# A row maximum that ignores NaN on one core: the loads of tiles 6 to 60 split into two halves on two DMA queues

## The chip, the core and the metric

The kernel runs on one core of a Trainium2 chip. Four engines matter. VectorE (DVE) does the reductions, ScalarE (ACT) and GpSimd (POOL) do passes over the elements, SyncE (SP) issues DMAs; the core's 16 DMA engines carry the transfers between the memory of the chip (HBM) and the on-chip memory (SBUF). TensorE is not used. Each engine runs its own list of instructions in order, and engines wait for each other on semaphores. The metric is the device time of one execution in microseconds; before the change it is 1252.5 us (median of 3 runs, 1252.5 to 1252.64).

## What is computed

```python
batch, seq, dim = 32, 2048, 2048
x = np.random.randn(batch, seq, dim).astype(np.float32)
mask = np.random.rand(batch, seq, dim) < 0.1
x[mask] = np.nan

def reference(x, axis):            # axis is -1
    return np.nanmax(x, axis=axis).astype(np.float32)
```

There are 65,536 rows of 2048 float32, 537 MB in all, of which a tenth is NaN. The result is the largest number of each row with the NaNs left out, 65,536 numbers. Every element is read once from HBM.

## The kernel before, in words

**Tiles.** The input is cut into tiles that hold, in each of the 128 partitions, a run of whole or quarter rows: `Q = 512` elements is the unit, and a full tile has 28 of them per partition (7 rows, 57344 bytes in a partition, 7168 KB in all). `TILES` (line 16) lists for each tile its loads, its pieces and its reductions, in units. Tile 1 is small (4 units), tiles 2 to 62 are full and each come with one load, and from tile 63 on the loads are cut into ever smaller parts, so that little work is left after the last one. Tiles are numbered from 1 in this text.

**The work on a tile.** A NaN has to be taken out before the maximum. Three steps do that, each with its own engine:
- ACT makes keys: for each piece it reads the upper 16 bits of every element as int16 and writes a u16 key into one of three key buffers `kt` (line 384). The function is a Prelu whose two slopes map bit patterns of numbers and of NaNs onto separate ranges.
- POOL turns the keys back and writes them over the upper 16 bits in the tile `xt` (line 405), which leaves NaNs as bit patterns that lose in a maximum. A negative number of units in the list of pieces means that ACT does this step too for that piece (`held` and `release`, line 357); in the middle of the kernel this is so in one tile of eight, the first of them tile 9.
- DVE reduces whole rows of the tile to their maxima in `acc` (line 430).

In the profile all of ACT's and all of POOL's passes have the line of their helper (L222, L232), and DVE's reductions have L239.

**Rows without a number.** A row of NaNs alone would keep a value at the lower end; `find` (line 241) corrects such entries of `acc` in one pass on DVE (L245), with `acc` as both tensor inputs. It is called behind tile 60 for 414 columns and behind the last tile for 7. For the fifth group `find_late` (line 256) does it on POOL in two instructions.

**Buffers and order.** Three tile buffers `xt` and three key buffers `kt` are used in turn. `Order` writes the waits: each instruction raises a semaphore of its engine (a DMA one of its own lane by 16), and `add` puts a wait before an instruction for each dependency that the engine has not yet seen. Each engine's list is in the order in which the Python code adds to it. A load waits for `free` of its buffer (line 311), which is the last reduction of the tile three before it:

```python
xt, before = xts[number % BUFS], free[number % BUFS]
...
free[(number - 1) % BUFS] = after[-1:]
```

All loads and the stores at the end are issued by SP, in order, on SP's queue. The first piece of a tile waits for the load that holds it. A key pass waits for POOL, where the key buffer that it writes is still being read (`kold`).

Of the kernel before, what the change touches and what calls it, by code (L numbers as in the profile page):

```python
# [10 lines left out]
Q = D // 4  # L11
# [38 lines left out]
GROUPS = [TILES[i : i + 15] for i in range(0, 60, 15)] + [TILES[60:73], TILES[73:]]  # L50
# [3 lines left out]
LATE = 4  # L54
# [3 lines left out]
BUFS = 3  # L58
# [4 lines left out]
LEAD = 128  # L63

LANES = 14

# [9 lines left out]
def total(pieces):  # L78
    return sum(sum(map(abs, p)) if isinstance(p, tuple) else abs(p) for p in pieces)
# [93 lines left out]
def kernel(  # L173
# [15 lines left out]
    nc = tc.nc  # L189
    P = nc.NUM_PARTITIONS  # L190
    f32, i32 = mybir.dt.float32, mybir.dt.int32
    i16, u16 = mybir.dt.int16, mybir.dt.uint16
    ALU = mybir.AluOpType
# [6 lines left out]
    xr = x.bitcast(i32).flatten_outer_dims()  # L200
    R = xr.shape[0]
    of = out.bitcast(i32).flatten_outer_dims().rearrange("r c -> (r c)")
    rows = [sum(sum(loads) for loads, _, _ in g) * Q // D for g in GROUPS]
    assert R == P * sum(rows)

    sing = ctx.enter_context(tc.tile_pool(name="sing", bufs=1))

    scalars = sing.tile([P, LEAD // 4], f32, name="scalars")
    warm = scalars[:, 1:2]
    xts = [sing.tile([P, WIDE * D], i32, name=f"xt{i}") for i in range(BUFS)]  # L210
    kts = [sing.tile([P, KEYS], u16, name=f"kt{i}") for i in range(NKEYS)]
    accs = sing.tile([P, sum(rows)], f32, name="acc")
    late = sing.tile([P, rows[LATE]], i32, name="late")

    with tc.tile_critical():  # L215
# [25 lines left out]
        def find(deps, acc):  # L241
            return order.add(
                "dve",
                nc.vector,
                lambda: nc.vector.scalar_tensor_tensor(  # L245
                    out=acc,
                    in0=acc,
                    scalar=LEAST,
                    in1=acc,
                    op0=ALU.is_ge,  # L250
                    op1=ALU.mult,
                ),
                deps,
            )

        def find_late(deps, acc, none):
            e = order.add(
                "pool",
                nc.gpsimd,
                lambda: nc.gpsimd.tensor_scalar(  # L260
                    out=none,
                    in0=acc,
                    scalar1=LEAST,
                    scalar2=float(0x00400000),
                    op0=ALU.is_lt,
                    op1=ALU.mult,
                ),
                deps,
            )
            bits = acc.bitcast(i32)  # L270
            return order.add(
                "pool",
                nc.gpsimd,
                lambda: nc.gpsimd.tensor_tensor(out=bits, in0=bits, in1=none, op=ALU.add),  # L274
                [e],
            )

# [15 lines left out]
        turn = 0  # L293
        stores = []
        ready = []
        flagged = 0
        r0 = 0
        for gi, (s, g) in enumerate(zip(rows, GROUPS)):
# [6 lines left out]
            for loads, pieces, reds in g:  # L305
# [2 lines left out]
                number += 1  # L308
                landed = []
                at = 0  # L310
                for c in loads:
                    c *= Q
                    e = order.add(
                        "sp",
                        nc.sync,
                        lambda: nc.sync.dma_start(  # L316
                            out=xt[:, at : at + c], in_=xg[:, base + at : base + at + c]
                        ),
                        before + lanes[turn],
                        lane=f"load{turn}",  # L320
                        step=16,
                    )
                    lanes[turn] = [e]
                    turn = (turn + 1) % LANES
                    landed.append((at, at + c, e))
                    at += c
                clean = []
                after = []
                at = done = 0
# [27 lines left out]
                def release():  # L357
                    for a, b, k, kp, e, i in held:
                        e = act(
                            [e],  # L360
                            name(i),
                            out=xt[:, a:b].bitcast(i16)[:, 1::2],
                            in_=kp,
                            func=ACT.Copy,
                            bias=float(TOP),
                            scale=-1.0,
                        )
                        cleaned(a, b, k, i, e)
                    held.clear()

                for parts in pieces:
                    parts = parts if isinstance(parts, tuple) else (parts,)
                    c = int(sum(map(abs, parts))) * Q
                    here = [l for a, b, l in landed if a < at + c and b > at]
                    kold = []
                    if used + c > KEYS:
                        key = (key + 1) % NKEYS
                        used = 0
                        kold, kfree[key] = last(kfree[key]), []
                        assert all(k != key for q in half.values() for _, _, k, _, _ in q)  # L380
                        if at + c == sum(loads) * Q:

                            kold = kold + last(kfree[(key + 1) % NKEYS])
                    e_key = act(
                        here + kold,
                        out=kts[key][:, used : used + c],
                        in_=xt[:, at : at + c].bitcast(i16)[:, 1::2],
                        func=ACT.Prelu,
                        bias=EDGE,
                        scale=-1.0,  # L390
                        alpha=float(TOP - LOW) / (EDGE - NAN),
                    )
                    release()
                    for c in parts:
                        back, wait, c = c < 0, isinstance(c, float), int(abs(c)) * Q
                        kp = kts[key][:, used : used + c]
                        used += c
                        to = xt[:, at : at + c].bitcast(i16)[:, 1::2]
                        at += c
                        if back:  # L400
                            held.append((at - c, at, key, kp, e_key, piece))
                            if not wait or at == sum(loads) * Q:
                                release()
                        else:
                            e = pool(
                                [e_key],
                                name(piece),
                                out=to,
                                in0=kp,
                                scalar1=-1.0,  # L410
                                scalar2=float(TOP),
                                op0=ALU.mult,
                                op1=ALU.add,
                            )
                            cleaned(at - c, at, key, piece, e)
                        piece += 1
                        open_ = [h[0] for h in held] + [p[0] for q in half.values() for p in q]
                        while reds and done + reds[0] <= min([at] + open_):
                            n = reds.pop(0)


                            lo = done - 1 if done % D else done
                            done += n
                            row = (base + lo) // D
                            if done % D:
                                m, to = 1, xt[:, done - 1 : done].bitcast(f32)
                            else:
                                m = max(n // D, 1)
                                to = acc[:, row : row + m]
                            e = dve(  # L430
                                [e for a, b, e in clean if b > lo and a < done] + part,
                                nc.vector.tensor_reduce,
                                out=to,
                                in_=xt[:, lo:done]
                                .bitcast(f32)
                                .rearrange("p (c d) -> p c d", c=m),
                                axis=mybir.AxisListType.X,
                                op=ALU.max,
                            )
                            part = [e] if done % D else []  # L440
                            after.append(e)
# [8 lines left out]
            if gi == LATE:  # L450
                late_acc = accs[:, lo:flagged]
            else:
                e = find(after, accs[:, lo:flagged])
                ready += [e] * (gi + 1 - len(ready))
            if gi == len(GROUPS) - 1:
                ready[LATE] = find_late(late_after, late_acc, late)
        for (og, bits), e in zip(stores, ready):
            last = order.add(
                "sp",
# [44 lines left out]
```

## Time and profile before

| | us |
|---|---|
| median of 3 runs | 1252.5 |
| the profiled execution's own time | 1252.48 |
| its span (first to last instruction) | 1250.7 |
| POOL busy | 1168.5 (93%) |
| DVE busy | 1111.4 (89%) |
| ACT busy | 965.6 (77%) |
| packets of queue q1, share of 16 DMA engines' span | 99.4% |
| HBM read | 536.87 MB, 429 GB/s over the span |

The span is one profiled execution. Busy time is what an engine spent in its instructions; issuing a DMA is not counted. q1 is the queue of the loads and stores that SP issues; q14 carries fetches of instructions. The chain is followed back from the last instruction, at each step to what released it. A row of a group reads: line, engine, operation, what is written from what, shapes, count, busy us, mean ns of one, idle time before and who ended it. A window row holds its length, then the busy time of DVE, ACT and POOL with the number of instructions, then the TensorE clock, the DMA share and the GB/s.

### The profile page before, as it was taken

The numbers are of one execution on the slowest core, as the hardware profiler recorded it, in microseconds if no ns is written. First come the engines' busy times: TensorE is split into PE (matmuls) and PEld (weight loads), VectorE is DVE, ScalarE is ACT, GpSimd is POOL, SyncE is SP. The second block draws the span as 40 slices with busy tenths as digits, with TensorE's granted clock in tenths as the row PEclk, the third lists the DMA queues.
The fourth block names the chain that finished last, engine by engine and source line by source line (L and its number), as shares of the span: only waits on it lengthen the run. The fifth ranks groups of instructions, "written<-read, shape, count | busy, mean of one in ns | idle before, by whom it ended". The sixth has DMA issues, their size and how long they took to land.

```text
span 1250.7 us, 891 instructions
## 1 busy us (share of the span) xinstructions
DVE 1111.4 (89%) x179; ACT 965.6 (77%) x273; POOL 1168.5 (93%) x242
## 2 busy tenths in 40 slices
DVE  0888989888889888898988888998888899999999
ACT  3777887778777877788777877777777778999997
POOL 2999989998999899998999899999999999989998
DMA  9999999999999999999999999999999999999997
GB/s 415 440 418 433 440 440 438 413 440 440 440 433 418 440 440 438 429 424 440 440 436 424 431 440 438 436 424 433 440 438 435 422 436 436 425 434 429 431 428 301
DMA packets 15991, 537.20 MB, mean 430 GB/s; under 512 B 2544, under 2 KB 2544, under 8 KB 3568
## 3 DMA queue, kind: packets, MB, share of 16 engines
q1 hardware_dynamic: 15984, 537.14, 99.4%
q14 instruction: 7, 0.06, 0.0%
HBM read 536.87 MB, written 0.26 MB: 429 GB/s over the span
## 4 chain that ended last, share of the span: by engine, by line
DMA 40%; DVE 29%; POOL 22%; ACT 9%; issue 1%; SPq 0%
DMA xt<-in_x_dram 40%; DVE acc L239 29%; POOL xt L232 22%; ACT kt L222 8%; ACT xt L222 1%; SPq L316 0%; DVE acc L245 0%; SPq L499 0%; SPq L215 0%
## 5 line engine op out<-in xcount | busy, mean ns | idle before, releaser
L232 POOL TENSOR_SCALAR xt<-kt 128x3584 int16<-128x3584 uint16 (+11 forms) x236 | 1167.4, 4947 | 77.6 <-ACT kt L222 63.9
L239 DVE TENSOR_REDUCE acc<-xt 128x3 f32<-128x6144 f32 (+4 forms) x175 | 1107.5, 6379 | 135.6 <-POOL xt L232 128.1
L222 ACT ACTIVATE kt<-xt 128x3584 uint16<-128x3584 int16 (+9 forms) x247 | 913.4, 3734 | 278.0 <-DMA xt<-in_x_dram 257.9
L222 ACT ACTIVATE xt<-kt 128x512 int16<-128x512 uint16 (+6 forms) x24 | 52.8, 2202 | 0.7
L245 DVE SCALAR_TENSOR_TENSOR acc<-acc 128x414 f32<-128x414 f32 (+1 forms) x2 | 2.2, 1111 | 0.1
L222 ACT ACT_TABLE_LOAD x1 | 1.3, 1283 | 0.9 <-SPq L215 0.9
L239 DVE TENSOR_REDUCE xt<-xt 128x1 f32<-128x1536 f32 x1 | 1.7, 1743 | 0.0
L278 DVE MEMSET scalars<- 128x1 f32 x1 | 0.1, 59 | 1.0 <-SPq L215 1.0
L260 POOL TENSOR_SCALAR late<-acc 128x91 int32<-128x91 f32 x1 | 0.5, 549 | 0.1
L274 POOL TENSOR_TENSOR acc<-acc,late 128x91 int32<-128x91 int32 x1 | 0.3, 341 | 0.1
L485 POOL MEMSET const-float32-0.0<- 128x1 f32 x1 | 0.1, 98 | 0.2 <-issue 0.2
L222 ACT ACTIVATE scalars<-scalars 128x1 f32<-128x1 f32 x1 | 0.2, 203 | 0.0
L485 POOL MEMSET const-bfloat16-1.0<- 128x1 bf16 x1 | 0.1, 101 | 0.0
L485 POOL MEMSET const-uint8-127<- 128x1 uint8 x1 | 0.1, 101 | 0.0
L485 POOL MEMSET const-float32-1.0<- 128x1 f32 x1 | 0.1, 98 | 0.0
## 6 DMA issues: line engine op xcount, KB each, us to landing
xt<-in_x_dram SPq DMA_DIRECT2D x61, 7168.0 KB, 22.6
xt<-in_x_dram SPq DMA_DIRECT2D x2, 5120.0 KB, 17.4
xt<-in_x_dram SPq DMA_DIRECT2D x3, 2816.0 KB, 22.7
xt<-in_x_dram SPq DMA_DIRECT2D x4, 2048.0 KB, 22.3
xt<-in_x_dram SPq DMA_DIRECT2D x5, 1536.0 KB, 29.1
xt<-in_x_dram SPq DMA_DIRECT2D x2, 3584.0 KB, 24.8
xt<-in_x_dram SPq DMA_DIRECT2D x6, 1024.0 KB, 26.8
xt<-in_x_dram SPq DMA_DIRECT2D x3, 1792.0 KB, 30.1
```

The costliest lines, as they stand in the source:

```text
L222: lambda: nc.scalar.activation(**kw),
L232: lambda: nc.gpsimd.tensor_scalar(**kw),
L239: return order.add("dve", nc.vector, lambda: do(**kw), deps)
L245: lambda: nc.vector.scalar_tensor_tensor(out=acc, in0=acc, scalar=LEAST, in1=acc, op0=ALU.is_ge, op1=ALU.mult,),
L260: lambda: nc.gpsimd.tensor_scalar(out=none, in0=acc, scalar1=LEAST, scalar2=float(0x00400000), op0=ALU.is_lt, op1=ALU.mult,),
L274: lambda: nc.gpsimd.tensor_tensor(out=bits, in0=bits, in1=none, op=ALU.add),
L278: e_warm = order.add("dve", nc.vector, lambda: nc.vector.memset(warm, 1.0), [])
L485: nc = _bacc.Bacc("TRN2", target_bir_lowering=False, num_devices=1)
```

## The change

From tile 6 to tile 60 (`SPLIT`, counted from 0 there) a load comes as two DMAs of 14 units each, 28672 bytes per partition. The front half is issued by SP where the whole load was issued. The rear half is issued by ACT, on a queue of ACT's own: behind the last key pass of a tile, ACT issues the rear of the tile two later, with a wait for the last reduction of the tile that held the buffer before. The two halves of a tile raise one of three semaphores (`half0` to `half2`) by 16 each, and the tile's passes wait for both. In tiles such as tile 9, the issue stands ahead of the pass that ACT does in POOL's place.

A second part: the correction behind tile 60 is done by DVE in two instructions in place of one. The first compares `acc` with the limit and writes a 32-bit pattern or zero into a new tile `none` in PSUM, the second ORs it into `acc`. The helper `find_late` becomes `find_apart`, with the engine and the operation as arguments; on POOL it does what it did.

```diff
+SPLIT = range(5, 60)
+HALF = 14
+HALVES = 3
...
+    flag = ctx.enter_context(
+        tc.tile_pool(name="flag", bufs=1, space=bass.MemoryType.PSUM)
+    )
...
+    nones = flag.tile([P, sum(rows[:LATE])], i32, name="none")
...
-        def find_late(deps, acc, none):
+        def find_apart(who, engine, deps, acc, none, op):
             e = order.add(
-                "pool",
-                nc.gpsimd,
-                lambda: nc.gpsimd.tensor_scalar(
+                who,
+                engine,
+                lambda: engine.tensor_scalar(
                     out=none,
                     in0=acc,
                     scalar1=LEAST,
...
             return order.add(
-                "pool",
-                nc.gpsimd,
-                lambda: nc.gpsimd.tensor_tensor(out=bits, in0=bits, in1=none, op=ALU.add),
+                who,
+                engine,
+                lambda: engine.tensor_tensor(out=bits, in0=bits, in1=none, op=op),
                 [e],
             )
...
+        halves = [[] for _ in range(HALVES)]
+        early = {}
+        plan = []
...
+        def load_half(t):
+            xg, base = plan[t]
+            h = halves[t % HALVES]
+            e = order.add(
+                "act",
+                nc.scalar,
+                lambda: nc.scalar.dma_start(
+                    out=xts[t % BUFS][:, HALF * Q : 2 * HALF * Q],
+                    in_=xg[:, base + HALF * Q : base + 2 * HALF * Q],
+                ),
+                free[t % BUFS] + h,
+                lane=f"half{t % HALVES}",
+                step=16,
+            )
+            halves[t % HALVES] = [e]
+            early[t] = e
...
+                if number - 1 in early:
+                    assert loads == [2 * HALF]
+                    name_ = f"half{(number - 1) % HALVES}"
+                    e = order.add(
+                        "sp",
+                        nc.sync,
+                        lambda: nc.sync.dma_start(
+                            out=xt[:, : HALF * Q], in_=xg[:, base : base + HALF * Q]
+                        ),
+                        before,
+                        lane=name_,
+                        step=16,
+                        joint=True,
+                    )
+                    halves[(number - 1) % HALVES] = [e]
+                    landed.append((0, 2 * HALF * Q, e))
+                    loads = []
...
+                    if number + 1 in SPLIT and at + c == done_at:
+                        load_half(number + 1)
                     release()
...
-                e = find(after, accs[:, lo:flagged])
+                acc = accs[:, lo:flagged]
+                if gi == len(GROUPS) - 1:
+                    e = find(after, acc)
+                else:
+                    e = find_apart("dve", nc.vector, after, acc, nones[:, lo:flagged], ALU.bitwise_or)
...
-                ready[LATE] = find_late(late_after, late_acc, late)
+                ready[LATE] = find_apart("pool", nc.gpsimd, late_after, late_acc, late, ALU.add)
```

## The prediction

> **What bounds the kernel now.** Tiles are numbered from 1, as in the change. I read four views: the DMA queues, the stretches, the waits with the chain, and the instructions in order of time. Queues first:
>
> ```profile
> span 1250.7 us, 891 instructions
> ...
> q1 hardware_dynamic: 15984, 537.14, 99.4%
> q14 instruction: 7, 0.06, 0.0%
> ```
>
> All loads go through one queue, q1, which keeps the 16 DMA engines busy for 99.4% of the span. Then the stretches (length, busy us of DVE, ACT, POOL, clock, DMA share, GB/s):
>
> ```profile
> 50.00:1030.00 980.00, 876.80 (x117) 740.85 (x180) 938.27 (x170) 1.00 1.00 434
> 1030.00:1058.00 28.00, 27.97 (x6) 23.43 (x6) 27.57 (x5) 1.00 1.00 434
> 1058.00:1140.00 82.00, 81.84 (x15) 77.14 (x26) 74.86 (x17) 1.00 1.00 432
> 1237.00:1251.00 14.00, 11.07 (x6) 7.88 (x8) 8.88 (x8) 1.00 0.38 141
> ```
>
> The DMA share is 1.00 from 50 us to the tail. In 50 to 1030 us no engine is full (POOL 96%, DVE 89%, ACT 76%); from 1030 us on DVE is full too (81.84 of 82). So the loads set the pace up to tile 62, and from there DVE runs without a gap worth naming behind an anchor that the loads set. The waits say the same from the engines' side:
>
> ```profile
> ACT kt L222 <- DMA xt<-in_x_dram: 257.9, 69, 15.0
> DVE acc L239 <- POOL xt L232: 128.1, 58, 23.0
> ```
>
> ACT, which reads a tile first, waits for its landing 69 times. In order of time (start, length, idle before):
>
> ```profile
> 56.47 7.12 ACT L222 ACTIVATE kt<-xt 128x3584 uint16<-128x3584 int16 x2 [4.16 <-DMA xt<-in_x_dram]
> 59.74 16.73 POOL L232 TENSOR_SCALAR xt<-kt 128x3584 int16<-128x3584 uint16 x3 [0.26 <-ACT kt L222]
> 63.96 5.32 ACT L222 ACTIVATE kt<-xt 128x6144 uint16<-128x6144 int16 x1 [0.37 <-POOL xt L232]
> ...
> 73.38 7.12 ACT L222 ACTIVATE kt<-xt 128x3584 uint16<-128x3584 int16 x2 [4.10 <-DMA xt<-in_x_dram]
> ...
> 90.27 7.12 ACT L222 ACTIVATE kt<-xt 128x3584 uint16<-128x3584 int16 x2 [4.06 <-DMA xt<-in_x_dram]
> ```
>
> Tiles 4, 5, 6 land 16.91 and 16.89 us apart. POOL works 16.73 of that, with 0.2 to 0.3 us to spare; ACT has 4 us. The chain shows how early a load is asked for:
>
> ```profile
> 52.39 15.16 DVE acc L239 x2
> 67.57 22.68 DMA xt<-in_x_dram
> 90.27 3.20 ACT kt L222
> ```
>
> Tile 6's load is issued at 67.57, when DVE has left its buffer, and tile 5 lands only at 73.38: the queue never runs dry, and the 5.8 us of lead is spare. In the trace's packet records a 57344-byte packet (one partition of a tile) takes 2116 ns, and its successor on the engine starts 3 ns before it ends. Eight of them and a semaphore packet (9 ns, spaced 6) make 8 x 2113 + 6 = 16,910 ns, exactly the landing interval.
>
> **The change part by part**, summed against the profiled execution: span 1250.7, 1252.48 us with what lies around it; the median of the runs, 1252.5, is the same number.
>
> *Smaller packets.* Each of 55 tiles now moves as 16 packets of 28672 bytes per engine and two semaphore packets. The trace has 256 packets of that size: 1062 ns. So 16 x 1059 + 2 x 6 = 16,956 ns, 46 ns more than before; 55 x 46 = +2.53 us on a full engine. This is not covered by anything: the share is 1.00, and the tail hangs on the landing of tile 62. The trace has no two data queues side by side, so bounds: from 8192 to 57344 bytes a packet's time grows by 1 ns per 27.2 bytes, which leaves 4.8 ns of each spacing that moves nothing. If the second queue hid these, a tile would take 8 x 57344 / 27.2 = 16,866 ns, 44 less than now: 55 x -44 = -2.4 us. The upper bound comes from q14. Six of its instruction fetches (8192 bytes, 309 or 314 ns) cut in between q1's packets while these ran. Going over to q14 cost nothing: the same 3 ns overlap. The first data packet of q1 behind it took 217 to 531 ns longer than its kind (median 244). At 217 ns for each of 16 switches a tile that would be 55 x 16 x 0.217 = +191 us; I hold that end unlikely, since the packet before the return was 309 ns short, and one of 1062 ns gives the next read three times that to start. I take +2.5: the step over to another queue is in all six cases spaced as one within q1.
>
> [...]
>
> *A second landing order.* A tile is ready when both halves are (one semaphore counts 32), so nothing starts earlier. The rear of tile n+2 is issued behind tile n's last key pass: tile 4 landed at 56.47, that pass ends at 69.28, +12.8 us. From the first issue to the first packet (0.96 to 1.96) went 1.0 us, so the rear reaches the engines at +13.8, up to 3.1 us before tile n+1 is in, and takes half of the engines from the front that is still missing. Tile n+1 can thus land up to 1.5 us late, the bytes going to the next tile instead. Lower bound 0, if the rears are not ahead. In the middle the 5.8 us of lead absorbs it. At the end it shows: tile 59 competes with rear 60, tile 60 with nothing. POOL would be up to 1.5 us late on tile 59 and wins back what it idles before tiles 60 to 62 (0.30, 0.16, 0.19 us): 0 to +0.8 at the anchor. I take +0.4, the middle, as no row prefers an end.
>
> *ACT issues 55 DMAs and waits for DVE in them.* A waiting issue takes 328 ns on SP; on ACT it falls into the 4 us before the next landing: 0. The wait is for tile n-1's last reduce: 67.54 against ACT's 69.28, over already; nearest is tile 58, 982.29 against 982.86. Queued behind is the key pass of the next tile, or in tiles such as 9 the pass that ACT does in POOL's place (153.78), for which DVE and then POOL wait: 0.33 us late five times, into 3.6 us that POOL idles there. If DVE ran 2 us later than now, ACT would stand still, and beyond 4 us POOL with it.
>
> *SP* keeps its order: fronts at the same places, one instruction each as before; loads of tiles 61 on and the stores are unmoved, 0.
>
> *The fixing of columns after tile 60.* One DVE pass with two SBUF inputs goes (2.06 us at 1032.58), two come, with an intermediate in PSUM. POOL's pass beside the old one took 7197 ns where the one of the tile before took 7040, and it is in the chain to the anchor: -0.15 if that meeting goes. DVE's own gain is worth nothing, as it then waits for POOL's end at 1058.47. [...] Sum here: -0.15.
>
> Sum: 2.53 + 0.4 - 0.15 = +2.8, **1255.3 us** (+0.22%). About 0.2%, 2.5 us, is what a measurement of this kernel can tell from no change.
>
> **The rivals.**
>
> *Hidden gaps (the other side).* While one queue's packet ends, the other's begins: all 4.8 ns and both semaphore packets vanish, -2.4, and with -0.15 and no lag at tile 59 it is 1249.9, just beyond 0.2%; with the lag of 0.4 it is 1250.3 and inside. It decides at 2.5 us, that is when the engines reach 27.2 bytes per ns. For it: nothing but the gap is left to win, and two queues are the obvious means. Against it: the unchanged spacing on the way to q14.
>
> *The return to a queue costs.* When a packet before a switch is short, the next read has no time to start. Semaphore packets are 9 ns, two a tile. One return a tile at 217 ns: 55 x 0.217 = +11.9, 1264; both at the median: 55 x 2 x 0.244 = +26.8, 1279. For it: all six returns. [...] It outweighs everything else from 50 ns a return. [...]
>
> *The queues are not served in turn.* If one is served first, only landings shift: at most half a tile, 8.5 us, once, beyond the lead of 5.8: up to +3 us, 1258. If the halves follow each other as one load did, the packets alone count and lag and gap stay out, 1254.9.
>
> **How the numbers follow.** Smaller packets in turn 0.42, of which two thirds end above 1255.0 (0.28 slower, 0.14 same). Hidden gaps 0.29: faster 0.17, same 0.12. Costly returns 0.23, slower. Queues not in turn 0.06, slower 0.04, same 0.02. Together: faster 0.17, same 0.28, slower 0.55. Low end 1249.7, just under the hidden gaps; high end 1268, through the one-return form of the third case with some more; its two-return form, about 0.12, and 0.05 below are left out. The likeliest case's own range is 1254.4 to 1256.5.
>
> **What would show it.** Right: two data queues with some half of the split bytes each; packets of 28672 bytes at about 1062 ns in turn; landings 16.95 us apart; POOL idle per tile up by 0.05; DVE still full from 1060 us. Hidden gaps would show as landings 16.87 apart; costly returns as packets behind a semaphore packet 200 ns and more too long, landings over 17.1 apart, GB/s under 430. ACT idle on DVE before its issues, or POOL's 7.2 us pass unchanged, would refute those steps. The prediction is wrong if engines move two queues' packets with an overlap other than 3 ns.

## The result, and the profile after

The changed kernel takes 1255.37 us (median of 13 runs, 1255.28 to 1255.62) against 1252.55 us for the kernel before on the same chip (13 runs, 1252.48 to 1253.34): a ratio of 1.0022 [1.0014, 1.003], 2.8 us slower. The profiled execution took 1255.3 us with a span of 1253.5 us; before it was 1252.48 and 1250.7.

The queues of the kernel after, from its page (a queue's line: packets, MB, share of the time of 16 DMA engines), and below them the issues of loads (count, KB each, median us from issue to landing):

```profile
span 1253.5 us, 947 instructions
...
q1 hardware_dynamic: 15984, 335.29, 62.2%
q10 hardware_dynamic: 7920, 201.85, 37.3%
q14 instruction: 8, 0.07, 0.0%
...
xt<-in_x_dram SPq DMA_DIRECT2D x57, 3584.0 KB, 21.1
xt<-in_x_dram ACTq DMA_DIRECT2D x55, 3584.0 KB, 22.7
```

There are now two data queues, and ACT's queue carries the 55 rear halves: 7920 packets are 55 x 16 engines x (8 of data and a semaphore). Together they fill 99.5% of the span, as q1 alone did. q14 has one fetch of instructions more, 8 instead of 7; that line turns out to matter.

The stretches of the kernel after (start and end, length, busy us of DVE, ACT and POOL, TensorE clock, DMA share, GB/s):

```profile
50.00:1030.00 980.00, 873.97 (x117) 738.62 (x179) 936.03 (x169) 1.00 1.00 433
1058.00:1140.00 82.00, 81.79 (x15) 77.43 (x25) 75.25 (x17) 1.00 1.00 432
1140.00:1200.00 60.00, 60.00 (x18) 55.43 (x25) 57.66 (x19) 1.00 1.00 428
```

In the middle the loads still set the pace (share 1.00), at 433 GB/s instead of 434, and each of the three engines does about 2.2 to 2.8 us less work in the same 980 us: the landings come later. DVE is full from 1058 us on, as before. Who waits for whom has not changed either (us in total, times, longest); no wait of ACT for DVE is among the waits:

```profile
ACT kt L231 <- DMA xt<-in_x_dram: 257.4, 67, 15.0
DVE acc L248 <- POOL xt L241: 131.5, 60, 23.0
```

ACT in order of time, with its DMA issues (ACTq; start, length, work, idle before and its releaser):

```profile
63.95 5.32 ACT L231 ACTIVATE kt<-xt 128x6144 uint16<-128x6144 int16 x1 [0.38 <-POOL xt L241]
67.60 0.39 ACTq L323 DMA_DIRECT2D xt<-in_x_dram  x1
74.39 7.12 ACT L231 ACTIVATE kt<-xt 128x3584 uint16<-128x3584 int16 x2 [5.11 <-DMA xt<-in_x_dram]
...
84.55 0.36 ACTq L323 DMA_DIRECT2D xt<-in_x_dram  x1
91.39 7.12 ACT L231 ACTIVATE kt<-xt 128x3584 uint16<-128x3584 int16 x2 [4.18 <-DMA xt<-in_x_dram]
...
108.29 7.12 ACT L231 ACTIVATE kt<-xt 128x3584 uint16<-128x3584 int16 x2 [4.07 <-DMA xt<-in_x_dram]
```

Two things are to be seen. Tile 5 lands at 74.39 instead of 73.38, a full microsecond late, and the next ones come 17.00 and 16.90 us apart. And the rear of tile 6 is issued at 67.60, while the key pass of 63.95 to 69.27 is still running: it follows that pass in ACT's program, but not in time. What releases it is the end of DVE's work on the buffer at 67.57.

The packet records of one DMA engine there (start in us, queue, kind, ns; T is 57344 bytes, H 28672, s a semaphore packet):

```
68.37 q1 T 2126 | 70.50 q1 T 2119 | 72.61 q10 H 1062 | 73.67 q1 s 9 | 73.68 q10 H 1062 |
74.73 q1 H 1062 | 75.79 q10 H 1062 | ... | 87.44 q1 H 1062 | 88.50 q10 s 9 | 88.50 q1 H 1062 |
89.56 q10 H 1062 | 90.62 q1 s 9 | 90.63 q10 H 1062
```

The engine serves the two queues strictly in turn, packet by packet, and a step to the other queue is spaced (1059 ns from start to start) exactly like one within a queue. From one semaphore packet of q1 to the next it is 16.95 us. Of the 14,336 packets of this size all take about 1062 ns, apart from 6, each behind a fetch on q14 (in two cases with one or two semaphore packets in between).

How far behind the kernel before the landings are (first key pass of the tile, after minus before):

| tile | 4 | 5 | 16 | 30 | 40 | 50 | 56 | 59 | 60 | 62 |
|---|---|---|---|---|---|---|---|---|---|---|
| us | -0.02 | +1.00 | +1.18 | +1.99 | +2.43 | +2.88 | +3.13 | +2.96 | +2.50 | +2.34 |

From tile 30 to tile 56 this grows by (3.13 - 1.99) / 26 = 0.044 us a tile. The extra lag that tile 5 picked up stays for as long as tiles are split and is gone at 62. DVE's anchor behind tile 62 starts at 1061.09 instead of 1058.51; by 1143 us the difference is down to +2.4 (DVE idled 0.12 us at 1140.72 in the kernel before and goes on without a gap now), and the landings of the last small loads are 2.3 us late up to 1210 us. Then half a microsecond is lost once more, at one instruction. Before:

```profile
1210.94 2.34 ACT L222 ACTIVATE kt<-xt 128x2560 uint16<-128x2560 int16 x1 [0.25 <-DMA xt<-in_x_dram]
...
1217.67 2.34 ACT L222 ACTIVATE kt<-xt 128x2560 uint16<-128x2560 int16 x1 [0.25 <-DMA xt<-in_x_dram]
```

and after:

```profile
1213.49 2.34 ACT L231 ACTIVATE kt<-xt 128x2560 uint16<-128x2560 int16 x1 [0.52 <-DMA xt<-in_x_dram]
...
1220.55 2.34 ACT L231 ACTIVATE kt<-xt 128x2560 uint16<-128x2560 int16 x1 [0.64 <-POOL xt L241]
```

The distance between the two kernels goes from +2.27 (the pass before these, 1207.84 against 1210.11) to +2.55 and +2.88. The first of these passes starts 0.32 us after its wait has ended, where it took 0.06 before. It is around the 319th instruction of ACT. Then, at 1216.80, q14 fetches 8192 bytes of instructions (309 ns on one DMA engine), and the data packet behind the fetch takes 633 ns where its kind takes 385. The kernel before has no fetch there. Its last reduction ends at 1247.91, the changed kernel's at 1250.74: +2.83, the measured difference.

### The profile page after: what moved, and what is told of

Read it like the earlier page. It is cut to its first block, busy times and chain, and to the rows that moved or that the text cites. A ratio compares the mean times of both kernels' runs of the same rounds, so it can differ in the third digit from the quotient of the medians.

```text
span 1253.5 us, 947 instructions
## 1 busy us (share of the span) xinstructions
DVE 1110.7 (89%) x180; ACT 965.5 (77%) x273; POOL 1169.1 (93%) x242
## 3 DMA queue, kind: packets, MB, share of 16 engines
q10 hardware_dynamic: 7920, 201.85, 37.3%
## 4 chain that ended last, share of the span: by engine, by line
DMA 54%; ACT 17%; POOL 15%; DVE 12%; issue 1%; SPq 0%; ACTq 0%
DMA xt<-in_x_dram 54%; ACT kt L231 17%; POOL xt L241 15%; DVE acc L248 12%; ACT xt L231 0%; SPq L371 0%; DVE acc L254 0%; SPq L561 0%; ACTq L163 0%; SPq L224 0%
```

## The experiments

Two theories went in. *Packets*: the 46 ns a tile of smaller packets make the 2.5 us, and the rest is small change from the landing order and the correction pass. *Queues and place*: some of the 2.8 us belongs to the second queue or to ACT as its issuer. Later the question was what the last half microsecond is. Diffs are against the changed kernel where nothing else is said. Times are medians; "tile 62" is how far later it lands than in the kernel before.

**find_only: the correction in two passes alone, no load split**

```diff
-SPLIT = range(5, 60)
+SPLIT = range(0)
```

> Only the second part of the change: loads as before, the correction behind tile 60 in two DVE instructions through PSUM. My sum: landings as before; POOL's pass beside the correction back from 7.20 to 7.04 us, so at most 0.15 us earlier at the end: 1252.35 to 1252.55 us. Rival, that this pair costs time of its own and explains part of the +2.8: 1252.8 us or more, with DVE's reductions of tile 61 starting later than before.

1252.61 us (11 runs, 1252.42 to 1252.8), ratio 1.0 [0.9991, 1.0008]. DVE of this kernel in order of time:

```profile
1032.92 0.59 DVE L269 TENSOR_SCALAR none<-acc 128x414 int32<-128x414 f32 x1
1033.54 0.59 DVE L283 TENSOR_TENSOR acc<-acc,none 128x414 int32<-128x414 int32 x1
1034.63 23.80 DVE L248 TENSOR_REDUCE acc<-xt 128x4 f32<-128x8192 f32 x4 [0.50 <-POOL xt L241]
1058.86 6.55 DVE L248 TENSOR_REDUCE acc<-xt 128x3 f32<-128x6144 f32 x1 [0.43 <-POOL xt L241]
```

The pair takes 1.18 us instead of 2.06, and POOL's pass beside it is back to its usual length. What DVE saves it then waits for POOL, and what POOL saves it waits for ACT, which waits for tile 62. POOL before:

```profile
1028.35 13.18 POOL L232 TENSOR_SCALAR xt<-kt 128x5120 int16<-128x5120 uint16 x2 [0.16 <-ACT kt L222]
1041.72 23.31 POOL L232 TENSOR_SCALAR xt<-kt 128x4096 int16<-128x4096 uint16 x4 [0.19 <-ACT kt L222]
```

and in this kernel:

```profile
1028.69 13.03 POOL L241 TENSOR_SCALAR xt<-kt 128x5120 int16<-128x5120 uint16 x2 [0.17 <-ACT kt L231]
1042.07 23.32 POOL L241 TENSOR_SCALAR xt<-kt 128x4096 int16<-128x4096 uint16 x4 [0.34 <-ACT kt L231]
```

13.18 and 0.19 us make the same as 13.03 and 0.34. The interval of the ratio, 1 us to each side, could not tell the prediction's -0.15 from 0; these rows can, and it is 0.

**both_sp: both halves issued by SP on q1, nothing by ACT**

```diff
-                if number - 1 in early:
+                if number - 1 in SPLIT:
...
+                    e = order.add(
+                        "sp",
+                        nc.sync,
+                        lambda: nc.sync.dma_start(
+                            out=xt[:, HALF * Q : 2 * HALF * Q],
+                            in_=xg[:, base + HALF * Q : base + 2 * HALF * Q],
+                        ),
...
-                    if number + 1 in SPLIT and at + c == done_at:
-                        load_half(number + 1)
```

> The same halves, front and rear, but both issued by SrcE's neighbour SP on the one queue, ACT issues nothing. Theory that each packet costs its engine 4.8 ns on whichever queue: tile 62 lands 2.3 to 2.5 us later than before, tile 5 lands on time (no rear packet gets ahead of its semaphore), POOL and DVE follow; 1254.8 us, 0.3 to 0.6 under the changed kernel, because ACT has no additional instructions to fetch. Rival, that the second queue is what costs: landings as before, 1252.4 us.

1254.87 us (11 runs, 1254.65 to 1254.98), ratio 1.0017 [1.0008, 1.0026]. Its queues, and ACT in order of time:

```profile
q1 hardware_dynamic: 23904, 537.14, 99.5%
q14 instruction: 7, 0.06, 0.0%
```

```profile
73.33 7.13 ACT L231 ACTIVATE kt<-xt 128x3584 uint16<-128x3584 int16 x2 [4.09 <-DMA xt<-in_x_dram]
...
90.25 7.13 ACT L231 ACTIVATE kt<-xt 128x3584 uint16<-128x3584 int16 x2 [4.09 <-DMA xt<-in_x_dram]
```

With all packets in one queue tile 5 is on time (73.33; before 73.38), yet tile 62 is 2.48 us late, just as with two queues. So the 2.3 us that are left come from the packets alone, and the late tile 5 from the second queue. 0.5 us of the change is missing here.

**quarters: each half as two DMAs on the same queue, packets of 14336 bytes**

```diff
-            e = order.add(
-                "act",
...
+            for i in (2, 3):
+                u, v = i * HALF * Q // 2, (i + 1) * HALF * Q // 2
+                e = order.add(
+                    "act",
+                    nc.scalar,
+                    lambda: nc.scalar.dma_start(
+                        out=xts[t % BUFS][:, u:v], in_=xg[:, base + u : base + v]
+                    ),
...
+                    for i in (0, 1):
+                        u, v = i * HALF * Q // 2, (i + 1) * HALF * Q // 2
```

> Each half as two DMAs, so 32 packets of 14336 bytes and four semaphore packets per engine and tile, two queues. Theory of 4.8 ns a packet: 32 x 532 + 4 x 6 = 17048 ns a tile, 138 more than before, tile 62 lands 7.6 us late; 1260.3 us with 0.5 in the tail. Rival, that changes of queue cost and not packets: twice the changes, twice the 2.3 us, 1257.5 us. Rival, that a load in parts costs something fixed: 1255.4 us.

1260.23 us (4 runs, 1260.02 to 1260.28), ratio 1.006 [1.0044, 1.0075]. Its queues:

```profile
q1 hardware_dynamic: 23904, 335.29, 62.2%
q10 hardware_dynamic: 15840, 201.86, 37.5%
```

The step from 8 to 16 packets a tile and engine cost 2.4 us at tile 62; from 8 to 32, three times the step, costs 7.20 us. What these runs paid goes with the number of packets, across two queues (+2.34 and +7.20 us at tile 62) as in one (+2.48 in both_sp).

**old_find: the changed kernel with the old correction pass**

```diff
-                if gi == len(GROUPS) - 1:
+                if True:
                     e = find(after, acc)
```

> The changed kernel with the old correction behind tile 60, one DVE pass of 2.06 us. By the sum in the prediction, 0.15 us more than the changed kernel (POOL's pass beside it back at 7.20 us), 1255.5 us. By what the run with the correction alone showed, DVE and POOL wait again before 1145 us and the difference is gone by then: 1255.4 us.

1255.31 us (11 runs, 1255.18 to 1255.56), ratio 1.0023 [1.0014, 1.0032]: no difference from the changed kernel. The correction is worth nothing in either company.

**pad_act: the kernel before, with 55 instructions more on ACT**, each a wait that is long fulfilled, where the change has its issues. Against the kernel before:

```diff
+                    if 3 < number < 59 and at + c == total(pieces) * Q:
+                        nc.scalar.wait_ge(order.sems["dve"], 1)
```

> The kernel before with 55 semaphore waits that are long fulfilled, put on ACT where the change has its rear issues; no DMA is touched. In the changed kernel the tail has one instruction fetch more (1216.80 us), and landings after 1210 us are 0.3 to 0.6 us later than the packets explain. Theory that the 55 instructions bring this fetch and it delays one DMA engine: a fetch near 1214 us, landings after it 0.2 to 0.5 us late, 1252.7 to 1253.0 us. Rival, that the tail's loss comes from the halves: 1252.5 us.

1253.24 us (11 runs, 1253.03 to 1253.82), ratio 1.0005 [0.9996, 1.0014]. The interval of the ratio still takes in 1; the median is 0.65 us above that of the kernel before in the same session (1252.59). ACT in the tail:

```profile
1211.34 2.34 ACT L222 ACTIVATE kt<-xt 128x2560 uint16<-128x2560 int16 x1 [0.54 <-DMA xt<-in_x_dram]
...
1218.27 2.34 ACT L222 ACTIVATE kt<-xt 128x2560 uint16<-128x2560 int16 x1 [0.51 <-DMA xt<-in_x_dram]
```

The loss in the tail is there without any split load: 0.54 instead of 0.25 us of idle time at the same pass, a fetch at 1214.52, and +0.60 at the later one. In the traces ACT's fetches come some 128 of its instructions apart (61, 189 and 317 had started at them in pad_far): ACT has 299 in the kernel before and 354 in the changed one, and 55 more bring one more fetch into the run.

**both_sp_pad: both_sp with the same 55 instructions on ACT** (the diff is against both_sp)

```diff
+                    if 3 < number < 59 and at + c == done_at:
+                        nc.scalar.wait_ge(order.sems["dve"], 1)
```

> Both halves on SP, and 55 fulfilled waits on ACT where the change has its issues: the packets and ACT's number of instructions as in the changed kernel, but one queue. Theory that the 0.5 us between the changed kernel and both halves on SP is ACT's boundary in the tail: 1255.2 to 1255.5 us. Rival, that it is the second queue or the later landings that come with it: 1254.9 us.

1255.35 us (11 runs, 1255.28 to 1255.76), ratio 1.0022 [1.0013, 1.003]: the changed kernel's time, and 0.48 above both_sp, whose slowest run (1254.98) is below the fastest here. ACT's tail in this kernel:

```profile
1213.59 2.34 ACT L231 ACTIVATE kt<-xt 128x2560 uint16<-128x2560 int16 x1 [0.52 <-DMA xt<-in_x_dram]
...
1220.59 2.34 ACT L231 ACTIVATE kt<-xt 128x2560 uint16<-128x2560 int16 x1 [0.58 <-DMA xt<-in_x_dram]
```

One queue, and still the changed kernel's time and its tail. So what two queues cost over one is not the queue. It is ACT's 55 instructions, whatever they are.

**split_pad, pad_more, pad_far, split_far: does it matter where the extra block is fetched?** My theory was that the fetch costs because it falls into the tail, behind which nothing is left to win the time back; moved to an earlier place it should be absorbed. More fulfilled waits on ACT move it. split_pad and split_far are the changed kernel with

```diff
                         load_half(number + 1)
+                        for _ in range(2 if number < 34 else 1):    # split_far: 3
+                            nc.scalar.wait_ge(order.sems["dve"], 1)
```

and pad_more and pad_far the kernel before with

```diff
+                    if 3 < number < 59 and at + c == total(pieces) * Q:
+                        for _ in range(3 if number < 34 else 2):    # pad_far: 5, 3
+                            nc.scalar.wait_ge(order.sems["dve"], 1)
```

> The changed kernel with 85 more fulfilled waits on ACT, spread over tiles 4 to 58. Theory that ACT pays about 0.3 us, and a fetch on a DMA engine, each time it passes a multiple of some 128 instructions, and that the 55 issues put the third of these into the tail (instruction 319, at 1213 us): the third now falls before 1030 us, where ACT has 4 us to spare per tile; from 1205 us on landings are no later than the packets make them; 1254.8 to 1255.0 us, 0.4 to 0.5 less than the changed kernel, with more instructions. Rival, that the number of ACT's instructions or its queue in itself costs: 1255.4 us or more.

> The kernel before with 140 fulfilled waits on ACT in place of the 55 of the run that took 1253.24 us. Theory that it is the place of ACT's block boundary and not the number of its instructions that costs in the tail: the boundary falls before 1030 us and the next one beyond the end, so 1252.5 to 1252.75 us, 0.5 less than with 55. Rival, that more instructions cost more, in whatever place: 1253.3 us or more.

> Two such waits in a row share one instruction, so the run with 140 of them had 85 instructions more and its boundary (instruction 319) came at 1156 us, not before 1030. This one has 140 instructions more, the boundary at about 985 us, where ACT has 4 us to spare, and none after it. Theory that the place in the tail costs: 1252.5 to 1252.75 us. Rival, that one more block costs wherever it is fetched, since the fetch holds up one DMA engine for about 0.55 us that it never wins back: 1253.0 to 1253.2 us, with the landings of tile 62 already 0.2 us or more late against tile 2.

> The changed kernel with 85 instructions more on ACT (the earlier attempt had 55, and its boundary at 1095 us); the boundary falls at about 1000 us. Theory of the place: 1254.8 to 1255.0 us. Rival, one more block costs wherever it is: 1255.3 us.

Two waits in a row turned out to share one instruction in the trace, so that fewer were added than written: 55 in split_pad, 85 in pad_more and split_far, 140 in pad_far.

| | ACT's instructions | the extra fetch at | us (runs, range) | ratio |
|---|---|---|---|---|
| split_pad | 409 | 1095.57 | 1255.32 (10, 1255.22 to 1255.52) | 1.0023 [1.0014, 1.0032] |
| pad_more | 384 | 1156.33 | 1253.14 (11, 1252.97 to 1253.48) | 1.0004 [0.9995, 1.0013] |
| pad_far | 439 | 965.76 | 1253.48 (11, 1253.15 to 1253.82) | 1.0007 [0.9998, 1.0016] |
| split_far | 439 | 972 | 1256.17 (7, 1255.63 to 1256.77) | 1.0028 [1.0017, 1.0039] |

None of them is measurably lower than the same kernel with its fetch in the tail (1255.37 and 1253.24). The two with 439 instructions are even higher, by 0.2 and 0.8; of that 0.3 lies outside the span (2.1 us there instead of 1.8), and the rest of split_far's has no explanation here. In split_pad the stumble at 1213 us has gone from the trace, and the time has not. (The expectations of split_pad and pad_more supposed a fetch before 1030 us, which these two did not get.) split_pad also parts the fetch from the number of instructions: it has 55 more on ACT than the changed kernel, no fetch more, and the same time. How the loss looks in the middle is seen in ACT's order of time, first in pad_far, whose fetch is at 965.76, then in pad_more, which has none there:

```profile
953.41 7.12 ACT L222 ACTIVATE kt<-xt 128x3584 uint16<-128x3584 int16 x2 [3.93 <-DMA xt<-in_x_dram]
...
971.01 12.39 ACT L222 ACTIVATE kt<-xt 128x3584 uint16<-128x3584 int16 x3 [4.73 <-DMA xt<-in_x_dram]
```

```profile
953.41 7.12 ACT L222 ACTIVATE kt<-xt 128x3584 uint16<-128x3584 int16 x2 [3.94 <-DMA xt<-in_x_dram]
...
970.31 12.39 ACT L222 ACTIVATE kt<-xt 128x3584 uint16<-128x3584 int16 x3 [4.04 <-DMA xt<-in_x_dram]
```

Up to 953.41 the two agree to the digit. Across the fetch the landings are 17.60 us apart instead of 16.90. What was lost there is not won back: in pad_far tile 62 is still 0.55 us late. The theory of the place is refuted.

Which DMA engine a fetch holds up can be read from the packet records: on each engine a packet starts 3 or 4 ns before the one ahead of it ends, so that an engine's packets can be put in a row. In pad_far the fetches at 186.82, 542.47 and 965.76 fall on one and the same engine. They are ACT's, of which 61, 189 and 317 instructions had started by then. Each takes 309 ns, and the packet behind it 242 to 250 ns more. The fetches at 254.32 and 998.86 fall on another engine, the one at 385.63 on a third. A tile is in when its last engine is (tile 5 of the kernel before: 16 semaphore packets end from 72.54 to 73.01 us, the key pass starts at 73.38). At ACT's third fetch its engine is the last already, so the next landing comes 17.46 us after the one before it instead of 16.91: the whole 0.55 counts. In the kernel before, the five fetches from 248 to 999 us fall on three engines and move the landings by 0.19 (248 and 254 together), 0.33, 0.22 and 0.00 us, 0.74 in all. Not every fetch cost half a microsecond in these traces; ACT's third did.

**by_parts: the halves cut by partition**, 0 to 63 by SP and 64 to 127 by ACT, so that packets keep their 57344 bytes and only the queues are two

```diff
-                    out=xts[t % BUFS][:, HALF * Q : 2 * HALF * Q],
-                    in_=xg[:, base + HALF * Q : base + 2 * HALF * Q],
+                    out=xts[t % BUFS][P // 2 :, : 2 * HALF * Q],
+                    in_=xg[P // 2 :, base : base + 2 * HALF * Q],
...
-                            out=xt[:, : HALF * Q], in_=xg[:, base : base + HALF * Q]
+                            out=xt[: P // 2, : 2 * HALF * Q],
+                            in_=xg[: P // 2, base : base + 2 * HALF * Q],
```

> The halves are cut by partition: SP loads partitions 0 to 63, ACT 64 to 127, so packets stay at 57344 bytes, eight per engine and tile, with one semaphore packet more; two queues as in the change. Theory of the packets: 6 ns a tile, 55 x 6 = 0.3 us at the landing of tile 62, and 0.4 to 0.5 in the tail from ACT's instructions: 1253.2 us; tile 5 lands up to 2 us late, since a rear packet of 2.1 us comes ahead of its semaphore. Rival, that changing queues costs what the change lost (2.3 us for 16 changes a tile): half of it for eight, 1254.3 us. A third possibility is that 64 partitions on 16 engines land unevenly: slower by many us, with DMA share under 1.00.

2221.79 us (4 runs, 2218.76 to 2223.49), ratio 1.7737 [1.7713, 1.7761]. The middle of this kernel (columns as above):

```profile
50.00:1030.00 980.00, 447.87 (x60) 375.86 (x91) 476.24 (x86) 1.00 1.00 218
```

All DMA engines are busy all the time and move half: a packet of 57344 bytes takes 4266 ns instead of 2116, in strict alternation of the queues. As an answer on the second queue this is inconclusive, since something much larger took over. That something was not followed further by a run. The packet records have all 16 engines at packets of one and the same queue, that is of the same half of the partitions, at 1214 of 1500 instants between 300 and 1800 us, and the rate is 218 GB/s where the kernel before has 434; why is not shown by a run here.

**alternate: whole loads of 57344-byte packets, every second one by ACT on its queue**

```diff
-                    if number + 1 in SPLIT and at + c == done_at:
+                    if number + 1 in SPLIT[::2] and at + c == done_at:
                         load_half(number + 1)
...
-                    out=xts[t % BUFS][:, HALF * Q : 2 * HALF * Q],
-                    in_=xg[:, base + HALF * Q : base + 2 * HALF * Q],
+                    out=xts[t % BUFS][:, : 2 * HALF * Q],
+                    in_=xg[:, base : base + 2 * HALF * Q],
```

> Whole loads with 57344-byte packets, every second one of tiles 6 to 60 issued by ACT on its own queue at the place of the rear issues, the others by SP: two queues, packets as before. Theory of the packets: tile 62 lands as before, 0 to 0.1 us off; landings in between are up to two packets (4.2 us) late where the next tile's packets come in ahead; ACT has 327 instructions, so its boundary lies 8 before its end; 1252.5 to 1253.0 us. Rival, that a second queue costs by itself: 1253.5 us or more, with landing intervals over 16.92 us.

1271.54 us (5 runs, 1270.23 to 1274.89), ratio 1.0159 [1.0145, 1.0173], where no loss was expected. Its queues, and the middle:

```profile
q1 hardware_dynamic: 11952, 331.62, 61.3%
q10 hardware_dynamic: 4032, 205.52, 37.8%
```

```profile
50.00:1030.00 980.00, 860.37 (x115) 726.65 (x177) 920.02 (x166) 1.00 1.00 427
```

There are no more packets than in the kernel before, and 427 GB/s. The packet records of one engine show what happens:

```
155.32 q10 T 2116 | 157.44 q10 s 9 | 157.44 q1 T 2349 | 159.79 q1 T 2116 | ... |
174.58 q1 s 9 | 174.59 q10 T 2116 | ... | 191.50 q10 s 9 | 191.51 q1 T 2365
```

A load of one queue ends in its semaphore packet, and the next load begins in the other queue. The first data packet behind such a change can take some 250 ns longer: of 7808 full packets 527 are over 100 ns too long (median 253 ns, together 13.0 us for each of 16 engines), against 6 in the kernel before. 28 loads by ACT make 56 changes on each of 16 engines, 896 in all. Where the packets are put in a row engine by engine, 381 of 873 changes, some four in ten, have such a packet directly behind the semaphore packet (median 263 ns), and these make 10.1 of the 13.0 us; the other long ones stand further back in a load or could not be placed. A tile is in when its slowest engine is, and tile 62 is 16.7 us late.

## Why the prediction came out where it did

It said 1255.3 us; the median is 1255.37. The total is right, and the largest term with it, but three smaller terms were off and cancelled each other; that the sum came within 0.1 us is luck.

- **Smaller packets, +2.53: right in mechanism and size.** In place of it the runs show +2.3 to +2.5 (both_sp: 2.28 in the medians, 2.48 at tile 62), 0.044 us a tile between tiles 30 and 56, and threefold with three times the added packets (quarters, +7.20). The step over to the other data queue has the same 3 ns of overlap, as it had towards q14. All three packet sizes agree: spacings of 2113, 1059 and 532 ns for 57344, 28672 and 14336 bytes leave 4.8 to 4.9 ns each beside 1 ns per 27.2 bytes, and in the changed kernel packets of q1 and of q10 alike take 1062 ns.
- **A second landing order, +0.4: the mechanism is there, the term is 0.** Tile 5 lands 1.0 us late with two queues and not with one, within the 0 to 1.5 that was named, and at tile 59 some 0.6 of the lag is left. At the end it is gone: tiles 60 to 62, which have nothing to share the engines with, are back at +2.3 to +2.5, the packets' own price. both_sp, without the lag, and both_sp_pad, which has the changed kernel's time without it, say the same of the time.
- **When the rear is issued: wrong, without consequence.** I put it at the end of tile n's last key pass, with the first packet 1.0 us later. The trace has the issue in the midst of that pass, at DVE's release (67.60), and the first packet 5.0 us later, behind two more packets of q1 (68.37 and 70.50). The pass and the issue follow each other in ACT's program; the issue did not wait for the pass to end.
- **ACT issues 55 DMAs, 0: wrong, it is +0.5.** I asked whether ACT had time for the issues, and it had: no wait for DVE appears, and no pass behind an issue mattered. What I did not count is the instructions themselves: there is one fetch of 8192 bytes more (1216.80), over DMA engines that have no time left, and on the one that held ACT's earlier fetches too (259.00 and 787.23). The prediction itself held the evidence, as it priced q14's fetches (309 ns, and 217 to 531 ns on the next packet) for another purpose. Here, where the loads leave the DMA engines no gap, the added fetch cost 0.48 us (both_sp to both_sp_pad).
- **The correction, -0.15: 0.** The sum has no delay from the pair on DVE, and there is none (1.18 us in find_only, where the old pass took 2.06); POOL's pass did go from 7197 to 7052 ns. The step that failed is that this pass sets the anchor: POOL then waits for tile 62, 0.34 us instead of 0.19 in find_only. That wait of 0.19 stands in the prediction, under another term. In old_find, too, no time comes of it.
- **SP, 0: right.** Its fronts stand where the whole loads stood; both_sp gives it 55 more issues and loses nothing that the packets don't explain.

So +2.5 + 0.4 + 0 - 0.15 = 2.8 was in truth about 2.3 + 0 + 0.5 + 0.

Of the rivals, *hidden gaps* is refuted: the spacing across the two queues is 1059 ns, not 1054, and the engines don't reach 27.2 bytes per ns. *The return to a queue costs* is refuted for this change and real elsewhere. In the split kernel both queues hold data at once, so that behind a semaphore packet (9 ns) of one queue comes a data packet of the other or of its own, and all but 6 of 14,336 are of normal length. In alternate, where a queue takes over from a finished one, the price is there in some four of ten changes, 263 ns where I had 217 to 244. Why is not shown: my argument that a data packet of 1 us ahead gives the next read time to start is an argument only, and it doesn't tell why some six in ten changes are free. *The queues are not served in turn* is refuted by the packet records.

Two things stay open: what the rest of split_far's time is, and how the last 0.3 us divides. The first landing alone (ACT's first key pass) varies between 5.57 and 5.99 us from kernel to kernel, and one profile of each can't tell terms below that apart. No kernel here is faster than the one before by more than can be measured.

## What to carry to other kernels

When the DMA engines are full, count what they must carry: here each packet cost 4.8 ns beside its bytes, and each fetch of instructions held up one DMA engine, by 0.55 us in the case of ACT's. That counted in full at 965.76 us in pad_far, where this DMA engine was the last one already; in the kernel before five fetches moved the landings by 0.74 us in all, the last of them by 0.00. A second queue changed the throughput neither way as long as both queues held data (433 GB/s in the middle, as in both_sp); handing whole loads back and forth between two queues cost some 260 ns at four changes in ten (alternate), and cutting loads by partition between them cost half the rate (by_parts, 218 GB/s). Where an edit adds instructions to an idle engine, ask not only whether that engine has time, but who fetches them.

## What the runs showed of the hardware that I had not expected

- In the changed kernel two queues with data were served packet by packet in strict turn on every DMA engine looked at: q1, q10, q1, q10, each 1059 ns after the other.
- Where whole loads alternate between two queues, the first data packet behind the other queue's semaphore packet took over 100 ns longer (median 263) in 381 of 873 changes (alternate).
- Two loads side by side, partitions 0 to 63 on one queue and 64 to 127 on the other, ran at 218 GB/s, with packets of 4266 ns instead of 2116 (by_parts).
- ACT's fetches, 8192 bytes each, came 128 of its instructions apart in pad_far (61, 189 and 317 had started), all over the same DMA engine; the third cost 0.48 us of the total (both_sp to both_sp_pad) although ACT is busy for only 77% of the changed kernel's span.
- A DMA issue of ACT was carried out while the pass ahead of it still ran (67.60 in 63.95 to 69.27), and two waits in a row ended up in one instruction (140 written, 85 more instructions in pad_more).
- A DVE pass over two inputs of 414 columns, beside POOL at work, took 586 ns where one of them lies in PSUM; the old pass with both in SBUF took 2.06 us and ended at 1034.64, 0.38 us after POOL's pass beside it. The operation differs too, so that PSUM alone makes the difference is not shown. From the page of the kernel after:

```profile
L269 DVE TENSOR_SCALAR none<-acc 128x414 int32<-128x414 f32 x1 | 0.6, 593 | 0.0
L283 DVE TENSOR_TENSOR acc<-acc,none 128x414 int32<-128x414 int32 x1 | 0.6, 586 | 0.0
```
